# RWKV-7 and chunk-attention block on one core: the solve's transfers on SP's queue, and one gate projection moved ahead

## The chip, the cores and the metric

The kernel runs on one core of a Trainium2 chip. The metric is device time in microseconds (us). The kernel before took 875.37 us (median of 3 runs, 874.01 to 878.43). The profile is one further execution of 873.35 us, of which the trace spans 871.6 us; 1.75 us lie around the span. All times "at 354.65" are us from the start of that span.

Engines: PE is the matrix engine (TensorE), DVE VectorE, ACT ScalarE, POOL GpSimd, SP the engine that does nothing but issue transfers. A transfer is issued by an instruction in the queue of SP or of ACT; an engine works its instructions off in order, so one that waits holds up all behind it.

## The reference

One layer of a residual block for 256 tokens of width 2048. The parts that matter here:

```
h = rms_norm(x)                                   # 256 x 2048
p_r, p_k, p_v, z_r, q, k, v, z_a, m_r, m_a = split(h @ w_in)
# branch 1, RWKV-7, 16 heads of 64: per token and head
sa    = state @ (-kk)
state = state * w + outer(sa, kk * a) + outer(v, k)
y     = state @ r
y_r   = (group_norm(y) * g + b + bonus) * silu(z_r)
# branch 2: attention in chunks of 64 with a relative bias, 16 heads
y_a   = attention(q, k, v) * silu(z_a)
merged = sigmoid(m_r + b0) * (y_r @ w_branch_rwkv) + sigmoid(m_a + b1) * (y_a @ w_branch_attn)
out    = x + rms_norm(merged @ w_out)
```

## The kernel before, in words

**Products.** Nearly all the work is a list of matrix products (`plan`), each read from HBM in weight chunks of 512 KB. `run_plan` walks the chunks. For each, SP loads `raw_*` (3 buffers), ACT copies it to `wh_*` (its high part, L81), DVE subtracts to get `wl_*` (the low part, L82; 4 buffers each), and PE multiplies both into an accumulator `acc_*` in PSUM. There are two accumulators, so a product can start only when that of the product before the last has been taken out (L383 on ACT, then L384 on DVE).

A product for a pair of 128 columns has four chunks. The names: `k`, `r`, `v` with a number are RWKV's inputs; `zr` its gate; `q`, `ak`, `va` the attention's inputs; `za` its gate. The number (0, 2, 4, 6) is the first 128-column tile j0, so `zr4` belongs to the third pair, and `raw_q23` in the order below is chunk 3 of q2. Then follow four rounds of `mr`, `ma`, `ur`, `ua` (merge gates and branch projections) and `o`. The string `ORDER` lists the products between `v6` and the merge: `z` stands for za, `v` for va, `q` for q and ak together, `r` for zr.

**The recurrence.** The 16 heads are two groups of eight; 256 tokens are four chunks of 64. `duo_front` prepares pairs; `group_back(g)` does the rest of a group:

- the solve: an inverse of (I - A) per head and chunk, first in 16 x 16 blocks. Eight small transfers of 16 KB put the diagonal blocks into `nb` in HBM (L577), one brings them back as `N` with another layout (L579), DVE forms the inverse row by row in `S` (15 steps, L590 and L592), one transfer writes `rb` (L595), and eight write the blocks into `R`, part of the tile `RA` (L599). Then come DVE's transpose `T` (L607) and PE's `z` (L611), DVE's `Z` (L615), PE's `xx` (L619), and a second level of the same (`z2`, `x2`; L628, L637).
- the chain over the four chunks c: on PE `pw` (L658, L662), `pu` (L668), `pg` (L682), `py` (L677, L685); on ACT `W`, `UV` and `Y` (L664, L671, L696); on DVE half of `UV` (L670) and the state `SB` (L693, L695).
- the group norm of `Y`.

The first solve falls at 142 to 199 us of the trace, the second at 317 to 379.

**What waits for what.** The q and ak of the third and fourth pair are taken into the tile `late`, which uses the memory of `A` of group 1; so they cannot be taken before group 1's chain has read `A` for the last time (L685 of the last chunk). The gate zr4 is taken into a tile of its own and has no such condition; it is multiplied with `Y` later (`gate`, L785).

**The order.** The code is written in generators (`side`, `back`) that are stepped after each chunk (`pump`), and then a scheduler that estimates times orders the instructions of every engine anew; what it gave is fixed in the program. What it gave is shown below. The engines run their queues in that order.

Of the kernel before, what the change touches and what calls it, by code (L numbers as in the profile page):

```python
# [32 lines left out]
FIRST = ((0, 2), (2, 2))  # L33


ORDER = "q0 r2 v0 z0 v1 r6 r0 z2 q2 q4 q6 z4 r4 z6"

P = 128
D = 2048
# [22 lines left out]
def kernel(ctx: ExitStack, tc, x, xt, vecs, w_in, wa1, w2, a2, w0, rel, w_br, w_ba, w_out, post_g, bm, out):  # L62
    nc = tc.nc
# [405 lines left out]
    def duo_front(j0):  # L469
# [92 lines left out]
        if q0:  # L562
            back.append(group_back(g))
            if g:
                back.append(start_att())

    def group_back(g):
        d = G[g]
        AB, A, UV = d["AB"], d["A"], d["UV"]
        Au = A.rearrange("p h j c a t -> p h (j c) a t")  # L570

        nb = dr.tile([2, 4, 16, 16, 16], F32, tag="nb", name=f"nb{g}")
        rb = dr.tile([2, 4, 16, 16, 16], F32, tag="rb", name=f"rb{g}")
        for h in range(2):
            for b in range(4):
                p0 = 64 * h + 16 * b
                nc.scalar.dma_start(nb[h, b].rearrange("u i j -> i u j"), Au[p0:p0 + 16, h, :, 0, 16 * b:16 * b + 16])  # L577
        N = tp.tile([P, 16, 16], F32, tag="Z2", name=f"N{g}", bufs=3)
        nc.scalar.dma_start(N.rearrange("p i j -> p (i j)"), nb.rearrange("h b u i j -> (h b u) (i j)"))  # L579
        S = tp.tile([P, 16, 16], F32, tag="Z2", name=f"S{g}", bufs=3)  # L580
        pr = tp.tile([P, 256], F32, tag="kk", name=f"pr{g}")
        POOL.memset(S, 0.0)
# [1 line left out]
        R = RA[0][:, 0:DB].rearrange("p (u t) -> p u t", u=16)  # L584
        POOL.memset(R, 0.0)
        yield
        for i in range(14, -1, -1):
# [4 lines left out]
            DVE.tensor_reduce(S[:, i, i + 1:16], pv, axis=AX.X, op=ALU.add)  # L592
            if i % 5 == 0:
                yield
        nc.scalar.dma_start(rb.rearrange("h b u i j -> (h b u) (i j)"), S.rearrange("p i j -> p (i j)"))  # L595
        for h in range(2):
            for b in range(4):
                p0 = 64 * h + 16 * b
                nc.scalar.dma_start(R[p0:p0 + 16, :, 16 * b:16 * b + 16], rb[h, b].rearrange("u i j -> i u j"))  # L599
        yield  # L600

        Rq = [R[:, q * 8:q * 8 + 8, :] for q in range(2)]
# [107 lines left out]
        for q in range(2):  # L710
            for m in range(2):
                jj = 2 * q + m
                j = 4 * g + jj
# [51 lines left out]
    def project_rkv(j0):  # L765
        def fresh():
            if j0 == 4:
                G[1] = group_new(1)
                side.append(group_decay(1))
        project(f"k{j0}", O_K + j0 * P, lambda acc: rkv(j0, 1)(acc), quota=QF, before=fresh, act=h_raw if j0 == 2 else h_norm)  # L770
        project(f"r{j0}", O_R + j0 * P, lambda acc: rkv(j0, 0)(acc), quota=QF)
        project(f"v{j0}", O_V + j0 * P, lambda acc: rkv(j0, 2)(acc), quota=QF)
# [150 lines left out]
    project_rkv(6)  # L923
    for what in ORDER.split():
        {"z": project_za, "v": project_va, "q": project_qk, "r": project_zr}[what[0]](int(what[1]))
# [152 lines left out]
```

## Time and profile before

| | us |
|---|---|
| median of 3 runs | 875.37 |
| profiled execution, whole | 873.35 |
| its span | 871.6 |
| PE busy | 846.0 (97% of the span) |
| DVE busy | 572.0 (66%) |
| ACT busy | 424.5 (49%) |
| POOL busy | 17.3 (2%) |

How to read it: PE is busy for all but about 25 us of the span. The busy time is a sum over stages; what a change to the order can move are the gaps in PE's row, and the stretches in which PE runs on a lower clock. Rows of the timeline give start, duration, engine, line and operation, and in brackets the idle time before and what ended it. A row with the engine `ACTq` or `SPq` is an instruction that issues a transfer.

### The profile page before, as it was taken

The page shows a single profiled execution, that of the slowest core. Times are in us where ns is not written, and L with a number is a line of the kernel's source. Part 1 is how long each engine was busy: PE and PEld are TensorE (multiplying, and loading weights), DVE is VectorE, ACT ScalarE, POOL GpSimd, SP SyncE. Part 2 cuts the span into 40 slices and gives each one's busy share as a digit, 9 for nine tenths or more (in the row PEclk, how much of TensorE's full clock was granted, in tenths as well). Part 3 has the DMA queues.
Part 4 walks back from the last instruction along what each step waited for, and adds up shares of the span by engine and source line. Part 5 has one row for each costly group of instructions (what it writes and reads, how often), then busy time and mean ns, then how long its engine had stood idle before and what let it go on. Part 6 is the DMA issues. An engine that isn't in the chain of part 4 may idle for free.

```text
span 871.6 us, 13996 instructions
## 1 busy us (share of the span) xinstructions
PE 846.0 (97%) x5624; PEld 716.5 (82%) x5624; DVE 572.0 (66%) x801; ACT 424.5 (49%) x600; POOL 17.3 (2%) x68
## 2 busy tenths in 40 slices
PE   8999999999999999899899999999999999999996
PEld 8998888888878888778687777888888888888896
DVE  7897995966548968544597774555564565555554
ACT  7557565446335545243456664444444444434442
POOL 2010000000010000000000000000000000000000
PEclk9999999999899999999999999999999999999999
DMA  9916644654243546534265445666666667675552
GB/s 294 252 53 181 191 138 142 193 159 124 76 141 98 186 145 212 180 101 133 86 188 164 132 129 176 209 195 198 205 193 200 208 194 230 209 260 198 194 192 97
DMA packets 119395, 149.35 MB, mean 171 GB/s; under 512 B 13601, under 2 KB 82209, under 8 KB 118946
## 3 DMA queue, kind: packets, MB, share of 16 engines
q1 hardware_dynamic: 105090, 138.43, 50.2%
q10 hardware_dynamic: 14240, 10.03, 4.0%
q8 instruction: 44, 0.72, 0.3%
q14 instruction: 21, 0.17, 0.1%
HBM read 145.82 MB, written 2.62 MB: 170 GB/s over the span
## 4 chain that ended last, share of the span: by engine, by line
PE 54%; DVE 1%; ACT 0%; DVEq 0%; issue 0%
PE acc_mr L275 10%; PE acc_ma L275 10%; PE acc_o L275 9%; PE acc_ua L275 5%; PE acc_ur L275 5%; PE acc_q L339 2%; PE acc_za L339 2%; PE acc_ak L339 2%; PE acc_q L337 1%; PE acc_za L337 1%; PE acc_ak L337 1%; PE acc_zr L339 1%; PE po L862 1%; PE acc_last L275 1%; PE pT L854 1%; PE pS L829 1%
## 5 line engine op out<-in xcount | busy, mean ns | idle before, releaser
L275 PE MATMUL acc_mr<-wh_mr,hn 128*128 128x512 f32 x256 | 82.0, 394 | 0.0
L275 PE MATMUL acc_ma<-wh_ma,hn 128*128 128x512 f32 x256 | 79.5, 389 | 0.0
L82 DVE TENSOR_TENSOR wl_ma<-raw_ma,wh_ma 128x1024 fp32r<-128x1024 f32 x32 | 39.2, 1224 | 42.3 <-ACT wh_ma L81 42.3
L82 DVE TENSOR_TENSOR wl_o<-raw_o,wh_o 128x1024 fp32r<-128x1024 f32 x31 | 37.9, 1225 | 32.9 <-ACT wh_o L81 32.9
L82 DVE TENSOR_TENSOR wl_mr<-raw_mr,wh_mr 128x1024 fp32r<-128x1024 f32 x32 | 39.1, 1223 | 28.8 <-ACT wh_mr L81 28.8
L275 PEld LDWEIGHTS acc_mr<-wh_mr,hn 128*128 128x128 f32 x256 | 47.8, 188 | 10.7 <-issue 1.2
L81 ACT ACTIVATE wh_ma<-raw_ma 128x1024 fp32r<-128x1024 f32 x32 | 34.0, 1061 | 46.3 <-PE acc_mr L275 20.9
L275 PEld LDWEIGHTS acc_ma<-wh_ma,hn 128*128 128x128 f32 x256 | 48.0, 188 | 10.0
L81 ACT ACTIVATE wh_mr<-raw_mr 128x1024 fp32r<-128x1024 f32 x32 | 33.9, 1060 | 43.3 <-PE acc_ua L275 19.9
L81 ACT ACTIVATE wh_o<-raw_o 128x1024 fp32r<-128x1024 f32 x31 | 32.9, 1060 | 39.0 <-PE acc_o L275 28.0
L275 PE MATMUL acc_mr<-wl_mr,hn 128*128 128x512 f32 x128 | 50.1, 392 | 0.0
L275 PE MATMUL acc_o<-wh_o,mgh 128*128 128x512 f32 (+1 forms) x140 | 49.9, 356 | 0.0
L275 PE MATMUL acc_o<-wl_o,mgh 128*128 128x512 f32 (+1 forms) x140 | 49.8, 356 | 0.0
L275 PE MATMUL acc_ma<-wl_ma,hn 128*128 128x512 f32 x128 | 49.8, 389 | 0.0
L275 PE MATMUL acc_va<-wh_va,hn 128*128 128x512 f32 x128 | 41.0, 398 | 0.0
L339 PE MATMUL acc_q<-hn,wh_q 128*128 128x512 f32 x128 | 33.8, 399 | 3.2 <-DVE late L384 1.7
L339 PE MATMUL acc_ak<-hn,wh_ak 128*128 128x512 f32 x128 | 33.9, 401 | 1.5 <-DVE aq L384 1.5
L339 PE MATMUL acc_za<-hn,wh_za 128*128 128x512 f32 x128 | 33.9, 398 | 0.0
L339 PE MATMUL acc_zr<-hn,wh_zr 128*128 128x512 f32 x128 | 33.3, 397 | 0.0
L82 DVE TENSOR_TENSOR wl_ua<-raw_ua,wh_ua 128x1024 fp32r<-128x1024 f32 x16 | 19.6, 1223 | 20.5 <-ACT wh_ua L81 20.5
L81 ACT ACTIVATE wh_ak<-raw_ak 128x1024 fp32r<-128x1024 f32 x16 | 16.7, 1056 | 31.5 <-PE acc_q L339 13.9
L82 DVE TENSOR_TENSOR wl_ur<-raw_ur,wh_ur 128x1024 fp32r<-128x1024 f32 x16 | 19.6, 1223 | 17.9 <-ACT wh_ur L81 17.9
(481 smaller groups left out, 2101.9 us busy)
## 6 DMA issues: line engine op xcount, KB each, us to landing
raw_mr<-w_in_d SPq DMA_DIRECT2D x32, 512.0 KB, 4.4
raw_ma<-w_in_d SPq DMA_DIRECT2D x32, 512.0 KB, 4.5
raw_o<-w_out_d SPq DMA_DIRECT2D x32, 512.0 KB, 3.7
raw_v<-w_in_d SPq DMA_DIRECT2D x16, 512.0 KB, 3.7
raw_q<-w_in_d SPq DMA_DIRECT2D x16, 512.0 KB, 4.6
raw_ak<-w_in_d SPq DMA_DIRECT2D x16, 512.0 KB, 3.7
raw_zr<-w_in_d SPq DMA_DIRECT2D x16, 512.0 KB, 3.7
raw_va<-w_in_d SPq DMA_DIRECT2D x16, 512.0 KB, 3.6
```

Source lines behind the costliest of these rows:

```text
L81: ACT.activation(h, src, AF.Copy)
L82: DVE.tensor_tensor(l, src, h.bitcast(F32), op=ALU.subtract)
L275: PE.matmul(d, u, v, start=first and n == 0, stop=last and n == len(ops) - 1)
L337: PE.matmul(acc[:, m, 0:256], wl[:, k, ms], a[:, 0, :], start=False, stop=g == ng - 1 and k == 3)
L339: PE.matmul(acc[:, m, :], wh[:, k, ms], a.rearrange("p n t -> p (n t)"), start=g == 0 and k == 0, stop=False)
L829: PE.matmul(pS[h][:, 128:384], q[HS[h], m, 128:256], k[HS[h], m, :], start=True, stop=True)
L854: PE.transpose(pT[:, b * P:(b + 1) * P], S[:, h, b * P:(b + 1) * P], ident)
L862: PE.matmul(po[m][HS[h], 128 * n:256], va[n][:, vc], att[1][:, 2 * m + h, c0:c1], start=not n, stop=bool(n))
```

## The change

It consists of two edits. The 18 transfers of each solve (`nb` x8, `N`, `rb`, `RA` x8) are issued by SP and no longer by ACT. And in `ORDER` the gate `r4` (product zr4, four chunks) stands ahead of q4 and ak4, where it stood between za4 and za6.

```
-ORDER = "q0 r2 v0 z0 v1 r6 r0 z2 q2 q4 q6 z4 r4 z6"
+ORDER = "q0 r2 v0 z0 v1 r6 r0 z2 q2 r4 q4 q6 z4 z6"
...
-                nc.scalar.dma_start(nb[h, b].rearrange("u i j -> i u j"), Au[p0:p0 + 16, h, :, 0, 16 * b:16 * b + 16])
+                nc.sync.dma_start(nb[h, b].rearrange("u i j -> i u j"), Au[p0:p0 + 16, h, :, 0, 16 * b:16 * b + 16])
...
-        nc.scalar.dma_start(N.rearrange("p i j -> p (i j)"), nb.rearrange("h b u i j -> (h b u) (i j)"))
+        nc.sync.dma_start(N.rearrange("p i j -> p (i j)"), nb.rearrange("h b u i j -> (h b u) (i j)"))
...
-        nc.scalar.dma_start(rb.rearrange("h b u i j -> (h b u) (i j)"), S.rearrange("p i j -> p (i j)"))
+        nc.sync.dma_start(rb.rearrange("h b u i j -> (h b u) (i j)"), S.rearrange("p i j -> p (i j)"))
...
-                nc.scalar.dma_start(R[p0:p0 + 16, :, 16 * b:16 * b + 16], rb[h, b].rearrange("u i j -> i u j"))
+                nc.sync.dma_start(R[p0:p0 + 16, :, 16 * b:16 * b + 16], rb[h, b].rearrange("u i j -> i u j"))
```

The scheduler gives a new order on all engines from the first solve on. Up to the first solve, and between the end of the first chain and the second solve, the order of PE is the one of before.

SP's queue at the second solve (`raw_q2x` and `raw_ak2x` are weight chunks of the products q2 and ak2):

```order
 L90 DMA raw_q22_4162<-w_in_d 128x4x256
 L90 DMA raw_q23_4185<-w_in_d 128x4x256
+L595 DMA rb1_2809<-S1_2820 128x256
+L599 DMA RA_848<-rb1_2809 16x16x16 x8
 L90 DMA raw_ak20_4207<-w_in_d 128x4x256
 L90 DMA raw_ak21_4229<-w_in_d 128x4x256
 L90 DMA raw_ak22_4254<-w_in_d 128x4x256
```

All four loads of ak2 now stand behind the nine transfers of the solve. At the first solve the pattern is nearly the same: rb, then raw_q02, then the eight RA, then raw_q03; and `nb` stands ahead of raw_r61, `N` behind it. On ACT these 36 rows are gone.

PE at the same place, the product q2 (chunks q20 to q23) with the solve's z and xx in between:

```order
 L339 MATMUL acc_q2_4166<-hn_656,wh_q21_4132 128x512 x8
 L337 MATMUL acc_q2_4166<-hn_656,wl_q21_4133 128x256 x8
+L611 MATMUL z10_2914<-T10_2912,A1_1878 64x64 x16
+L611 MATMUL z11_2933<-T11_2931,A1_1878 64x64 x16
 L339 MATMUL acc_q2_4166<-hn_656,wh_q22_4160 128x512 x8
 L337 MATMUL acc_q2_4166<-hn_656,wl_q22_4161 128x256 x8
-L339 MATMUL acc_q2_4166<-hn_656,wh_q23_4183 128x512 x8
-L611 MATMUL z10_2914<-T10_2912,A1_1878 64x64 x16
-L611 MATMUL z11_2933<-T11_2931,A1_1878 64x64 x16
-L337 MATMUL acc_q2_4166<-hn_656,wl_q23_4184 128x256 x8
+L339 MATMUL acc_q2_4166<-hn_656,wh_q23_4183 128x512 x2
 L619 MATMUL xx10_2974<-RA_848,Z10_2972 64x64 x16
```

The z of the second solve now stands after the second chunk of q2, where it stood in the fourth; xx comes after two matmuls of the fourth chunk, and z2 and the first of x2 move from within ak2 to ahead of it. At the first solve z moves ahead of the first chunk of q0, where it stood after five of its matmuls. On DVE, the last of the solve's 15 steps (`S`, L592) now stands ahead of the gate zr0 (L785) and of wl_q21; two chunks of wl_ak2 stand between `T` and `Z`, where three did.

PE at the end of group 1's chain, before (the last chunk of ak4 is just over):

```order
L658 MATMUL pw13_3389<-UV1_1879,A1_1878 64x64 x5
L662 MATMUL pw13_3389<-SB_162,AB10_1231 64x64 x4
L662 MATMUL pw13_3389<-SB_162,AB11_1232 64x64 x4
L668 MATMUL pu13_3408<-W13_3406,RA_848 64x64 x8
L677 MATMUL py13_3437<-AB10_1231,SB_162 64x64 x4
L677 MATMUL py13_3437<-AB11_1232,SB_162 64x64 x4
L685 MATMUL py13_3437<-A1_1878,UV1_1879 64x64 x8
L339 MATMUL acc_q6_4617<-hn_656,wh_q60_4565 128x512 x8
```

The same place in the changed kernel:

```order
L339 MATMUL acc_ak4_4624<-hn_656,wh_ak42_4618 128x512 x2
L668 MATMUL pu13_3408<-W13_3406,RA_848 64x64 x8
L677 MATMUL py13_3437<-AB10_1231,SB_162 64x64 x4
L677 MATMUL py13_3437<-AB11_1232,SB_162 64x64 x4
L339 MATMUL acc_ak4_4624<-hn_656,wh_ak42_4618 128x512 x6
L337 MATMUL acc_ak4_4624<-hn_656,wl_ak42_4619 128x256 x8
L339 MATMUL acc_ak4_4624<-hn_656,wh_ak43_4641 128x512 x6
L685 MATMUL py13_3437<-A1_1878,UV1_1879 64x64 x8
L339 MATMUL acc_ak4_4624<-hn_656,wh_ak43_4641 128x512 x2
L337 MATMUL acc_ak4_4624<-hn_656,wl_ak43_4642 128x256 x8
L705 MATMUL pvr10_3457<-ysq10_3455,onesb_108 128x256 x2
L339 MATMUL acc_q6_4715<-hn_656,wh_q60_4663 128x512 x8
```

Before, the chain's last chunk (names that end in 13) runs with no matmuls of a product in between; now its pieces stand between those of ak4. What follows is the same work with one product less: the attention of the third and fourth pair moves over into mr0 and ma0 by about the length of a product, and the last `po` (L862) from the end of mr0 into the first half of ma0.

## The prediction

> **What bounds the kernel now.** I read the page's busy times first, then the waits of PE, then the timeline of PE where it waits, then ACT, DVE and the transfers at those places.
>
> ```profile
> PE 846.0 (97%) x5624; PEld 716.5 (82%) x5624; DVE 572.0 (66%) x801; ACT 424.5 (49%) x600; POOL 17.3 (2%) x68
> ```
>
> ```profile
> PE pw L662 <- DVE SB L695: 3.2, 2, 2.2
> ```
>
> PE is idle for 25 us of 871.6, and the change neither adds nor removes a matmul. So the time moves only with PE's gaps behind the first solve, and with its clock. The head, up to 140 us, is untouched. The timeline of PE shows the gaps:
>
> ```profile
> 354.65 2.00 PE L339 MATMUL acc_q<-hn,wh_q 128*128 128x512 f32 x8
> ...
> 357.44 2.00 PE L339 MATMUL acc_q<-hn,wh_q 128*128 128x512 f32 x8
> 359.93 2.08 PE L611 MATMUL z<-T,A 64*64 64x64 f32 x64 [0.49 <-DVE T L607]
> ...
> 364.55 2.28 PE L619 MATMUL xx<-RA,Z 64*64 64x64 f32 x64 [1.39 <-issue]
> 368.35 2.14 PE L339 MATMUL acc_ak<-hn,wh_ak 128*128 128x512 f32 x8 [1.52 <-DVE aq L384]
> ...
> 386.62 2.12 PE L339 MATMUL acc_q<-hn,wh_q 128*128 128x512 f32 x8 [1.49 <-DVE ak L384]
> ...
> 408.83 0.69 PE L662 MATMUL pw<-SB,AB 128*64 128x64 f32 x16
> ...
> 420.45 1.13 PE L662 MATMUL pw<-SB,AB 128*64 128x64 f32 x16 [1.02 <-DVE SB L695]
> 422.05 0.68 PE L668 MATMUL pu<-W,RA 64*64 64x64 f32 x16 [0.47 <-ACT W L664]
> ...
> 426.03 2.11 PE L339 MATMUL acc_q<-hn,wh_q 128*128 128x512 f32 x8 [1.69 <-DVE late L384]
> ```
>
> Three groups: the second solve loses 0.49 + 1.39 + 1.52 = 3.40 us. The start of q4 loses 1.49. The end of the chain loses 1.02 + 0.47 + 1.69 = 3.18, and 0.44 more, as the pw of the last chunk takes 1.13 where it takes 0.69 between matmuls of a product. Why the second solve is late stands in the rows of ACT and DVE:
>
> ```profile
> 344.81 0.40 ACTq L818 DMA_DIRECT2D E<-rel_d  x1
> ...
> 346.30 0.33 ACTq L595 DMA_DIRECT2D rb<-S  x1
> ...
> 352.31 5.01 ACTq L599 DMA_DIRECT2D RA<-rb  x8
> 357.42 2.95 ACT L81 ACTIVATE wh_ak<-raw_ak 128x1024 fp32r<-128x1024 f32 x3 [8.00 <-DMA RA<-rb]
> ...
> 424.66 0.59 ACT L383 ACTIVATE late<-acc_q 128x512 f32<-128x512 f32 x1
> ...
> 425.62 1.16 ACT L702 ACTIVATE ysq<-Y 128x512 f32<-128x512 f32 x2
> ```
>
> ```profile
> 344.10 0.68 DVE L785 SCALAR_TENSOR_TENSOR zr<-Y,zr 128x512 f32<-128x512 f32 x1
> 344.70 1.22 DVE L82 TENSOR_TENSOR wl_q<-raw_q,wh_q 128x1024 fp32r<-128x1024 f32 x1
> 345.83 0.38 DVE L592 TENSOR_REDUCE S<-pr 128x15 f32<-128x225 f32 x1
> ...
> 359.17 1.30 DVE L607 STREAM_TRANSPOSE T<-RA 128x512 f32<-128x512 f32 x2 [8.49 <-DMA RA<-rb]
> 360.40 3.45 DVE L82 TENSOR_TENSOR wl_ak<-raw_ak,wh_ak 128x1024 fp32r<-128x1024 f32 x3
> ```
>
> The solve's inverse is done at 346.2, rb is issued at once, and RA waits 6 us for it to land, right behind the 512 KB of E on the same queue. ACT stands for 8.00 us with three copies wh_ak behind it. DVE stands for 8.49 us, then works off three wl_ak ahead of Z, for which xx waits. The transfers at both solves, the first from the window 165 to 182 us, the second from 344 to 360:
>
> ```profile
> raw_q<-w_in_d SPq DMA_DIRECT2D x4, 512.0 KB, 4.8
> rb<-S ACTq DMA_DIRECT2D x1, 128.0 KB, 3.2
> ```
>
> ```profile
> raw_ak<-w_in_d SPq DMA_DIRECT2D x3, 512.0 KB, 5.6
> E<-rel_d ACTq DMA_DIRECT2D x1, 512.0 KB, 5.7
> rb<-S ACTq DMA_DIRECT2D x1, 128.0 KB, 6.0
> ```
>
> **The change part by part. Second solve.** In the new order the last step of S stands ahead of the gate (0.68) and wl_q (1.22), so S ends at about 344.3. The nb are issued at the same time as before (they wait for A, not for a queue), so I leave the rest of the chain up to S alone. On SP, rb has raw_q23 ahead of it and E is on the other queue. How long rb takes there no row shows; I take the first solve's 3.2, where rb also had a raw_q in flight; the ends are 3.2 and 6.0. RA can then be issued at 347.5; eight take 5.0 us (352.31 row) and end at 352.5; T came 1.85 us after the last issue (359.17 - 357.32), so now at about 354.6, with the spread of my sum about 355. Half of T (0.65) is enough for the first z.
>
> PE reaches z earlier, since z now stands after the second chunk: at 354.65. It waits till 355.7, 1.0 us. Then z (2.08), chunk three (2.8, from 354.65 to 357.44) and two matmuls of the fourth (0.5): xx at 361.0.
>
> The price of the move is on SP: all behind RA waits. The loads of ak2 go out at 352.5 and no longer at 346 to 351. The first lands after about 4 us, the three within 5.6, so at 356.5 to 358.5; two copies of 1.06 and two wl of 1.23 later Z starts at about 360.3 and has its first half at 361.0. That is just in time: I put 0.5 us of waiting there. The take of aq still stands behind the fourth copy wh_ak on ACT, whose load needs the buffer of the first; so ak2 still waits, I say 1.0 us of the 1.52. Together 2.5 against 3.40: **0.9 us gained**. Ends: all gaps gone, 3.4 gained; or rb takes its 6.0 and T stays at 359.17: then z waits 5.2, and 2.8 us are lost.
>
> **Start of zr4 (before: of q4).** It needs the accumulator of ak2. In the old order nothing stood between, and PE waited 1.49. Now pg, py and the first pw of chunk 1 stand between, three times 16 small matmuls, 1.8 us at the 0.6 to 0.7 us that 16 take (408.83 row). ACT and DVE take ak2 in that time, after wl_zr43 (1.23) and with 0.69: 1.9 us. What is left is 0.2 to 0.3: **1.2 us gained**; ends 0 and 1.49.
>
> **End of the chain.** zr4 puts 11.2 us of matmuls (four chunks of 2.8) in front of q4, and its accumulator empties without waiting for `late`. So the last chunk of the chain runs between matmuls of ak4, and SB, W and UV have 2 us and more each. After the last py ten matmuls of ak4 are left (1.4 us); in that time ACT does Y, then late (0.59) and the first ysq (half of 1.16), and DVE its half of late (as long as the 0.68 of another 512-wide operation); pvr then covers the rest. I leave 0.3 us of waiting: 3.18 + 0.44 - 0.3 = **3.3 us gained**. Ends: 1.5, if late and ysq come in turn (1.69 stays), and 3.6.
>
> **First solve.**
>
> ```profile
> 151.78 0.16 DVE L590 TENSOR_TENSOR pr<-S,N 128x1 f32<-128x1 f32 x1 [1.68 <-DMA N<-nb]
> ...
> 180.44 1.30 DVE L607 STREAM_TRANSPOSE T<-RA 128x512 f32<-128x512 f32 x2 [1.22 <-DMA RA<-rb]
> ```
>
> ```profile
> 180.03 1.33 PE L339 MATMUL acc_q<-hn,wh_q 128*128 128x512 f32 x5
> 181.28 2.08 PE L611 MATMUL z<-T,A 64*64 64x64 f32 x64
> ```
>
> PE now reaches z at 180.03, 1.25 us earlier, and T was there at 181.1 (its first half). ACT no longer holds copies and takes behind nb, so S starts up to 1.7 us earlier and T comes at about 179.0 to 179.4: no wait. I take 0; if N and RA lose what they gain behind raw_r61 and raw_q02, z waits 1.1; if besides rb takes 6.0 instead of 3.2, 3.9. After this solve comes the longest gap, and the clock with it:
>
> ```profile
> 218.80 1.57 PE L662 MATMUL pw<-SB,AB 128*64 128x64 f32 x16 [2.16 <-DVE SB L695]
> ```
>
> ```profile
> 218.00:220.00 2.00, 1.14 (x15) 0.73 0.65 231
> 220.00:222.00 2.00, 1.53 (x24) 0.50 0.00 0
> 222.00:224.00 2.00, 2.00 (x37) 0.50 0.04 8
> 224.00:226.00 2.00, 2.00 (x34) 0.56 0.00 0
> ```
>
> Columns: length, PE busy (instructions), granted clock, transfers. 2 x (0.27 + 0.50 + 0.50 + 0.44) = 3.4 us are lost to the clock. DVE's work ahead of that SB (duo_front of the third pair) is the same in sum and merely swapped with wl_zr23, so gap and clock stay: 0, with 3.4 gained if the gap falls just short.
>
> **Cover.** All else that moves to SP costs nothing: 36 issues of 0.3 to 0.6 us while SP waits for buffers anyway; what hides it are three raw and four wh buffers, some 2.8 us each. The later attention is hidden as long as the last po and the gate of mr0 come before ur0.
>
> ```profile
> 528.38 0.87 PE L862 MATMUL po<-att_yrh,va 128*64 128x256 f32 x8
> ...
> 554.02 0.39 PE L275 MATMUL acc_ur<-wh_ur,yr_AB 128*128 128x512 f32 x1
> ```
>
> They are 25 us apart; the move takes some 11 to 14 of them.
>
> **Sum.** 0.9 + 1.2 + 3.3 = 5.4 us: the profiled execution's 873.35 would become 868.0, and the median of 875.37, which lies 2.0 above it, 870.0. About 0.5% (4.4 us) is what a measurement of this kernel can tell from no change.
>
> **A page's rule against the change.** That rb took 6.0 us behind E's 512 KB and 3.2 without is a row of this trace. The Trainium skill ("DMA: Bandwidth & Descriptors", Queues, rings and completion order) states that SP and ACT each own a row of rings on the same 16 engines, that a ring is worked in order and the engines take turns between rows. By that the solve's transfers lose their turns against the weight loads once they share SP's row, and it agrees with the 6.0 us. By it rb and RA would wait for the raw_q ahead of them, up to 4.8 us at each solve, and the sum would turn into the rival that follows.
>
> **The rivals.** *Solve stuck in SP's queue (slower).* Place: rb and RA of both solves behind raw_q23, raw_q01 and raw_q02. Price: with 6.0 for rb at both, 2.8 lost at the second and 3.9 at the first, and a z wait of 5.2 is longer than the 2.16 that brought the clock down, 3.4 more: 10.1 against the 4.5 of the other two terms, 5.6 slower, 881. It decides from T coming some 2.5 us later than I say at both solves. For it: the 6.0. Against: rb at the first solve had loads in flight and took 3.2, and at the second SP's queue holds one load, where ACT's held E. Its weaker form, only the second solve, costs 2.8, leaves 4.5 - 2.8 = 1.7 gained: 873.7, no change.
>
> *The clock keeps up at 219.* The gap is shorter by a few tenths and the drop does not come: 3.4 more, 866.6. For it: the gap is short. Against: nothing on DVE's path there gets less. The Trainium skill ("TensorE: Matmul & The Clock Gate", The HAM clock gate) puts the drop at one idle window of about 3.4 us; here 2.16 us of idling with another 0.47 behind it did it, so here the clock falls sooner than by the page, and I go by the trace.
>
> *zr4 does not help.* The chain's end stays bare, as DVE or ACT is late with SB or UV for another reason; then 3.3 becomes 0 to 1: 872.5. Against: the old gaps are there only where no product stands between.
>
> **How the numbers follow.** Forecast (4.4 to 8 gained) 0.50; clock kept too 0.09; one of the weaker cases (second solve gives back its part, or the chain's end half as good) 0.31; solve stuck at both 0.10. That gives faster 0.59, same 0.32, slower 0.09. Predicted 870.0; the likeliest case alone 867.5 to 871. The range 865.5 to 876 takes in the kept clock below and the weaker cases above, with the spread of the three runs.
>
> **What would show it.** Right: in the changed profile PE's wait at acc_q for late is below 0.5, no pw of the last chunk waits for SB, acc_zr starts with under 0.5, T of the second solve comes 3 to 5 us earlier and the wait of ACT for RA is gone. Wrong: z waits for T by more than 2 us, raw_ak or raw_q03 shows up as a releaser of PE, or a second stretch of half clock stands near 356.

## The result, and the profile after

The changed kernel took 863.21 us (median of 4 runs, 862.21 to 864.87), the kernel before 874.69 beside it (4 runs, 873.36 to 878.43): a ratio of 0.987, with a 95% interval of 0.985 to 0.989, so 1.3% or 11.5 us faster. The profiled executions differ by 9.83 us (873.35 and 863.52); the reading below accounts for those. I had forecast a gain of 5.4.

The page's line of busy times, then PE's waits behind the first solve:

```profile
PE 842.4 (98%) x5624; PEld 714.7 (83%) x5624; DVE 572.6 (66%) x801; ACT 425.4 (49%) x600; POOL 17.2 (2%) x68
```

```profile
PE pw L662 <- DVE SB L695: 1.8, 1, 1.8
...
PE pu L668 <- ACT W L664: 0.5, 1, 0.5
...
PE acc_ak L339 <- DVE aq L384: 0.3, 1, 0.3
PE acc_zr L339 <- DVE ak L384: 0.3, 1, 0.3
```

Two things are to be seen. The waits around the second solve and at the end of the second chain are gone but for 0.2 or 0.3 here and there; pw and pu are the gap behind the first solve, at 216.7, which stayed. And PE's busy time fell by 3.6 us with the same 5624 matmuls. My prediction allowed only for the 0.44 of one pw. Of the 3.6, 1.0 lies ahead of q2, where PE waits 1.3 us longer in this trace and nothing is gained; 2.8 lie between the starts of q6 and ur0, and these are gain; from q2 to q6 it rose by 0.2.

PE at the places of the prediction:

```profile
349.38 2.00 PE L339 MATMUL acc_q<-hn,wh_q 128*128 128x512 f32 x8
...
355.06 2.08 PE L611 MATMUL z<-T,A 64*64 64x64 f32 x64
...
360.53 2.19 PE L619 MATMUL xx<-RA,Z 64*64 64x64 f32 x64
...
367.40 2.08 PE L339 MATMUL acc_ak<-hn,wh_ak 128*128 128x512 f32 x8 [0.30 <-DVE aq L384]
...
385.02 2.14 PE L339 MATMUL acc_zr<-hn,wh_zr 128*128 128x512 f32 x8 [0.26 <-DVE ak L384]
...
428.06 0.69 PE L685 MATMUL py<-A,UV 128*64 128x64 f32 x16
...
431.01 2.21 PE L339 MATMUL acc_q<-hn,wh_q 128*128 128x512 f32 x8
...
445.96 2.00 PE L339 MATMUL acc_ak<-hn,wh_ak 128*128 128x512 f32 x8
...
544.26 0.39 PE L275 MATMUL acc_ur<-wh_ur,yr_AB 128*128 128x512 f32 x1
```

They are the starts of q2, z, xx, ak2, zr4, the last py, q6, ak6 and ur0. The starts of q2 and ak6 before, which are not shown yet:

```profile
349.06 2.00 PE L339 MATMUL acc_q<-hn,wh_q 128*128 128x512 f32 x8
...
442.19 2.00 PE L339 MATMUL acc_ak<-hn,wh_ak 128*128 128x512 f32 x8
```

Aligned at equal work (what PE has done more or less by then is added; zr4 is 11.17 us), the gain builds up as follows:

| from, to | gained, us | forecast |
|---|---|---|
| up to the start of q2 (the head differs from run to run) | -0.3 | 0 |
| q2 to the start of zr4: 386.62 against 385.02 (1.6), plus pg, py and pw, done by then (1.8), plus the 0.3 of the row above | 3.7 | 0.9 + 1.2 |
| to the start of q6: 426.03 against 431.01, zr4 and four pvr (0.8) done | 3.6 | 3.3 |
| to the start of ak6: 442.19 + 11.17 against 445.96 | 0.4 | 0 |
| to the start of ur0: 111.83 - 11.17 = 100.66 us before, 98.30 after | 2.4 | 0 |
| to the end | 0.0 | 0 |

The second solve on the transfers' side (DVE, SP, ACT; the numbers at the end of the last two rows are KB of one transfer and us from issue to landing):

```profile
343.82 0.38 DVE L592 TENSOR_REDUCE S<-pr 128x15 f32<-128x225 f32 x1
...
344.28 0.34 SPq L595 DMA_DIRECT2D rb<-S  x1
...
344.83 0.39 ACTq L818 DMA_DIRECT2D E<-rel_d  x1
...
347.87 3.77 SPq L599 DMA_DIRECT2D RA<-rb  x8
...
351.74 6.89 SPq L90 DMA_DIRECT2D raw_ak<-w_in_d  x4
...
353.60 1.30 DVE L607 STREAM_TRANSPOSE T<-RA 128x512 f32<-128x512 f32 x2 [2.60 <-DMA RA<-rb]
...
355.92 1.06 ACT L81 ACTIVATE wh_ak<-raw_ak 128x1024 fp32r<-128x1024 f32 x1 [6.18 <-DMA raw_ak<-w_in_d]
...
359.65 1.28 DVE L615 TENSOR_TENSOR Z<-z,m 128x512 f32<-128x512 f32 x2
```

```profile
rb<-S SPq DMA_DIRECT2D x1, 128.0 KB, 3.5
...
RA<-rb SPq DMA_DIRECT2D x8, 16.0 KB, 2.1
```

S ends at 344.20 and T starts at 353.60: 9.4 us, where it was 13.0 before (346.21 to 359.17). The raw_ak now go out behind RA; ACT waits 6.18 us for the first and DVE 2.11 for ACT's copy of it, but PE waits for neither.

### The profile page after: what moved, and what is told of

It reads as the page before. It is cut to its first block, busy times and chain, and to the rows that moved or that the text cites. A ratio compares the mean times of both kernels' runs of the same rounds, so it can differ in the third digit from the quotient of the medians.

```text
span 861.8 us, 14000 instructions
## 1 busy us (share of the span) xinstructions
PE 842.4 (98%) x5624; PEld 714.7 (83%) x5624; DVE 572.6 (66%) x801; ACT 425.4 (49%) x600; POOL 17.2 (2%) x68
## 4 chain that ended last, share of the span: by engine, by line
PE 93%; DVE 2%; DMA 2%; SPq 1%; issue 0%; ACT 0%; DVEq 0%
PE acc_mr L275 10%; PE acc_ma L275 10%; PE acc_o L275 10%; PE acc_va L275 5%; PE acc_ua L275 5%; PE acc_ur L275 5%; PE acc_zr L339 4%; PE acc_q L339 4%; PE acc_za L339 3%; PE acc_ak L339 3%; PE acc_v L339 3%; PE acc_r L339 3%; PE acc_za L337 2%; PE acc_zr L337 2%; PE acc_q L337 2%; PE acc_k L339 2%
## 5 line engine op out<-in xcount | busy, mean ns | idle before, releaser
L275 PEld LDWEIGHTS acc_ma<-wh_ma,hn 128*128 128x128 f32 x256 | 47.8, 188 | 10.1 <-issue 0.3
L82 DVE TENSOR_TENSOR wl_va<-raw_va,wh_va 128x1024 fp32r<-128x1024 f32 x16 | 19.5, 1222 | 17.2 <-ACT wh_va L81 15.8
```

The source lines that it names most:

```text
L82: DVE.tensor_tensor(l, src, h.bitcast(F32), op=ALU.subtract)
L275: PE.matmul(d, u, v, start=first and n == 0, stop=last and n == len(ops) - 1)
```

## The experiments

Times are medians beside the kernel before on the same chip; ratios are to it, with their 95% intervals. Times of stretches are of one profiled execution each. "Stretch" is the start of ak6 to the start of ur0, without zr4 where it lies in it.

**1. The two edits one at a time.** First the order alone:

```
-ORDER = "q0 r2 v0 z0 v1 r6 r0 z2 q2 q4 q6 z4 r4 z6"
+ORDER = "q0 r2 v0 z0 v1 r6 r0 z2 q2 r4 q4 q6 z4 z6"
```

> Only the order of the products is changed (zr4 ahead of q4); the solve's transfers stay on ACT. From the two traces the 9.8 us between them split into 2.7 at the second solve, 1.0 at the start of zr4, 3.6 at the end of the chain and 2.4 between the first ak6 and the first ur0, less 0.3 lost in the head. Theory one (order and queue add up, and the 2.4 belong to the order, as no pair of po stands split by a product any more): gains 1.0 + 3.6 + 2.4 = 7.0, so about 867.5 if the kernel before takes 874.5; ak6 to ur0 takes about 98.5 to 99.5 us without zr4's 11.2; E still stands ahead of rb on ACT and T of the second solve waits for RA. Rival (the 2.4 and part of the cover come from the transfers leaving ACT): gains 4.5 at most, 870, and ak6 to ur0 takes 100.7 without zr4. Rival two (the earlier zr4 is worth nothing while the solve stays on ACT): 873 to 875.

Measured 871.14 against 874.13, 0.9948 (0.9924 to 0.9972). PE's waits:

```profile
PE acc_q L339 <- DVE late L384: 1.7, 1, 1.7
PE acc_ak L339 <- DVE aq L384: 1.7, 1, 1.7
PE acc_zr L339 <- DVE ak L384: 1.5, 1, 1.5
```

Then the queue alone (the four lines `nc.scalar` to `nc.sync` of the change, with the old `ORDER`):

> Only the queue of the solve's transfers is changed to SP; the old order of products stays. Theory one: gains the second solve's 2.7 and nothing else, so about 871.8 against 874.5; rb of the second solve lands in 3.2 to 3.6 us in place of 6.0; the po pairs stay split and ak6 to ur0 keeps its 111.8 us. Rival (the transfers lose their turns behind the weight loads on SP): rb takes 5 us or more and the time is 874.5 or above. Rival two (the interleaving at the end comes from SP): 869.5 and ak6 to ur0 takes 109.5.

Measured 869.68 against 874.13, 0.9956 (0.9934 to 0.9978). PE's waits and the transfer:

```profile
PE acc_q L339 <- DVE late L384: 1.7, 1, 1.7
PE acc_ak L339 <- DVE aq L384: 0.3, 1, 0.3
PE acc_q L339 <- DVE ak L384: 0.3, 1, 0.3
```

```profile
rb<-S SPq DMA_DIRECT2D x1, 128.0 KB, 3.3
```

Neither theory fits whole. From the start of q2 to that of ur0 the order alone gains 3.7 us, the queue alone 5.3, both 10.1. The wait of 1.5 for ak2's take, which I had given to the order, goes with the queue: as the solve ends earlier, pg, py and pw of the chain stand ahead of the next product, whichever it is. The wait of 1.0 for SB at the chain's end goes with either edit, the wait for `late` only with both. With the order alone the last py stands behind all of ak4, which is over at 432.30, and ends at 432.92; with the queue alone no product is left either. Only an earlier chain and one product more give the ten matmuls of ak4 behind the last py; this I read from the orders, no run tries it by itself. The stretch takes 98.78 us with the order alone and 100.66 with the queue alone: that gain is the order's, as I had said.

**2. Why rb took 6.0 us.** My guess was E's 512 KB ahead of it on the same queue. So E goes to the other queue, in the kernel before:

```
-        nc.scalar.dma_start(E, bass.AP(rel.tensor, 2 * j0 * 513 + 129, [[1, P], [513, 4], [1, T]]))
+        nc.sync.dma_start(E, bass.AP(rel.tensor, 2 * j0 * 513 + 129, [[1, P], [513, 4], [1, T]]))
```

> The kernel before with one edit: the four loads E of the attention's bias (512 KB each) are issued by SP; the solve stays on ACT in the old order. Theory one (rb took 6.0 us because E stood ahead of it on the same queue): rb of the second solve lands in 3.2 to 3.8 us, T comes 2.2 to 2.8 us earlier (about 356.7), the waits of 0.49, 1.39 and 1.52 shrink by 2 us or more: 872 to 872.8 against 874.5. Rival (the 16 DMA engines were busy, whichever queue): rb stays at 5 to 6 us and the time at 874.5. Rival two (what costs is that ACT stands behind RA, not rb's landing): rb is faster but the gain is under 0.7.

Measured 873.59 against 874.13, 0.9995 (0.9978 to 1.0012), and:

```profile
rb<-S ACTq DMA_DIRECT2D x1, 128.0 KB, 5.9
```

The guess was wrong. Next, less traffic, again in the kernel before:

```
-        nc.scalar.dma_start(E, bass.AP(rel.tensor, 2 * j0 * 513 + 129, [[1, P], [513, 4], [1, T]]))
+        nc.scalar.dma_start(E[:, 0:4 if j0 else 1, :], bass.AP(rel.tensor, 2 * j0 * 513 + 129, [[1, P], [513, 4 if j0 else 1], [1, T]]))
```

> The kernel before, with the first E load cut from 512 to 128 KB: the first attention's four heads all take the bias of the first of them; nothing else is left out. With E on SP rb still took 5.9 us, so the queue ahead of rb is not its cause. Theory one (the traffic of two 512 KB loads in flight, E and the first raw_ak, slows rb whatever the queue): with one of them cut rb of the second solve lands in 3.5 to 4.5 us, T comes 1.5 to 2.5 us earlier, and 1 to 2 us are gained: 872 to 873 against 874. Rival (raw_ak alone is enough to slow rb, or ACT's queue is slow by itself): rb stays at 5.5 us or more, no gain.

Measured 873.77 against 874.56, 0.999 (0.9965 to 1.0015): rb became shorter as the first theory has it, but T came only 0.9 us sooner after the end of S, and no gain can be told. And the changed kernel, with RA alone back on ACT:

```
-                nc.sync.dma_start(R[p0:p0 + 16, :, 16 * b:16 * b + 16], rb[h, b].rearrange("u i j -> i u j"))
+                nc.scalar.dma_start(R[p0:p0 + 16, :, 16 * b:16 * b + 16], rb[h, b].rearrange("u i j -> i u j"))
```

> The changed kernel, with the eight RA loads of both solves issued by ACT again; nb, N and rb stay on SP. SP then no longer waits for rb and sends the four raw_ak right behind it. Theory one (what helps is that SP, in order, holds the raw_ak back until RA is out, so that rb and RA have the DMA engines nearly to themselves): rb takes 4.5 us or more at the second solve, RA is issued later than 348.5 less the shift of the head, eight issues take 5.0 instead of 3.8 us, and T comes 1.5 to 4 us later than in the changed kernel; 1 to 4 us of the gain are lost, 864.5 to 867. Rival (a small transfer is fast on SP, whatever runs beside it): rb 3.5, T within 1.3 us of the changed kernel's, and as wh_ak then no longer waits for its loads the time is 862.5 to 863.5.

Measured 866.38 against 874.56, 0.992 (0.9897 to 0.9943): some 2 to 3 us lost, as the first theory has it, but with an rb of 3.3 and not of 4.5 or more. The transfers of the second solve, first with a quarter of E, then with RA on ACT:

```profile
rb<-S ACTq DMA_DIRECT2D x1, 128.0 KB, 4.2
```

```profile
rb<-S SPq DMA_DIRECT2D x1, 128.0 KB, 3.3
RA<-rb ACTq DMA_DIRECT2D x4, 16.0 KB, 5.0
```

| kernel | in flight as rb is issued (us since their issue) | rb, us | last RA issue to T | end of S to T |
|---|---|---|---|---|
| before (rb on ACT) | E (1.5) on ACT, raw_ak (0.4) on SP | 6.0 | 1.9 | 13.0 |
| E on SP (rb on ACT) | E (1.5) and raw_ak (0.4) on SP | 5.9 | 1.7 | 12.8 |
| a quarter of E (rb on ACT) | 128 KB (1.5) on ACT, raw_ak (0.4) on SP | 4.2 | 3.3 | 12.1 |
| RA on ACT (rb on SP) | raw_q (1.4) on SP | 3.3 | 3.3 | 12.3 |
| queue alone | raw_q (1.4) on SP | 3.3 | 2.0 | 9.2 |
| changed | raw_q (1.4) on SP | 3.5 | 2.0 | 9.4 |

For rb, what decides is what was issued just ahead of it, and not on which queue: 6.0 and 5.9 with E on either, and 3.5 on SP right behind a load on SP. A load that follows rb counts less: in the three rows with rb on SP, E goes out on ACT 0.55 us behind rb, and rb still lands in 3.3 to 3.5. The traffic is paid for at rb or at RA: with a quarter of E, or with RA on ACT, the raw_ak that are then in flight go with a later landing of RA (3.3). It is paid least where SP, which works in order, stands at rb and RA and so holds the raw_ak back. RA on ACT releases them, and T comes 2.9 us later than in the changed kernel: 1.3 of that is the landing, and 1.9 that the eight issues take 5.66 us on ACT where they took 3.77 on SP. Whether ACT or the traffic makes the issues longer, no run separates. Of the gain, 1.7 us are lost between q2 and ur0 (1.0 against the second trace of the changed kernel, below). At the first solve and chain nothing is lost: from the start of v6 to that of va0 PE takes 72.53 us, and 72.65 in the changed kernel. The rest of the difference between the two medians I can't place.

**3. Where the busy time went.** In the old order PE's block of `po` was cut between its two heads at two places; in the new one it isn't. Before, at one of them:

```profile
486.34 0.65 PE L862 MATMUL po<-att_yrh,va 128*64 128x256 f32 x2
486.91 0.48 PE L827 MATMUL pS<-late 64*128 64x128 f32 x2
487.33 0.86 PE L862 MATMUL po<-att_yrh,va 128*64 128x256 f32 x6
```

The same block in the changed kernel:

```profile
484.88 0.87 PE L862 MATMUL po<-att_yrh,va 128*64 128x256 f32 x8
```

First try: the same eight matmuls, one head written behind the other.

```
-            for n, c0, c1 in ((0, 0, 256), (1, 256, 384)):
-                for h in range(2):
+            for h in range(2):
+                for n, c0, c1 in ((0, 0, 256), (1, 256, 384)):
```

> The changed kernel, with the two heads' po matmuls of a block written one head after the other, so that their two 64-row halves no longer follow each other directly. In the trace of before two of the eight blocks were cut between the halves by another matmul, and took 0.57 and 0.79 us, 1.36 together, where the uncut ones take 0.80. Theory one (two halves that follow each other directly run side by side, and each cut costs its 0.5 to 0.6 us on PE, which shows as busy time and not as a wait): eight blocks cost 0.5 to 0.6 more each, 4 to 5 in all: 867 to 868 against the changed kernel's 863.2; mr0 to ur0 gets longer and PE's busy time rises by as much. Rival (the lengths of such records are a matter of how ends are drawn, or the lost time is taken back in waits): within 1 us of 863.2.

Measured 864.94, 0.9897 (0.9875 to 0.9919), stretch 98.36: no difference from the changed kernel that can be told.

```profile
463.18 0.88 PE L862 MATMUL po<-att_yrh,va 128*64 128x256 f32 x8
```

The order of the heads is not what costs, as long as nothing comes in between. So the next kernel makes something come in between. The changed kernel stands beside it once more:

> The changed kernel itself, run beside the next two so that they can be compared with it on one chip: 863.2 against 874.5 for the kernel before, a ratio of 0.985 to 0.989; ak6 to ur0 98.3 us, T of the second solve 9.4 us after the end of S, as in its first trace.

Measured 864.12 against 874.75, 0.9878 (0.9855 to 0.9901); stretch 98.30. In this second trace z and xx of the second solve wait 0.3 and 0.5, where they waited for nothing in the first. The cut kernel (`turn_half` holds the transposes and the copy of one head; its definition, and the first head's call at the old place of the transposes, are left out here):

```
-            for n, c0, c1 in ((0, 0, 256), (1, 256, 384)):
-                for h in range(2):
+            for h in range(2):
+                if h:
+                    turn_half(m, 1)
+                for n, c0, c1 in ((0, 0, 256), (1, 256, 384)):
```

> The changed kernel, with each attention step's second head transposed (pT) only behind the first head's po matmuls, so that every po block falls in two pieces with product matmuls between, and pS and pT in smaller pieces too: 89 places where PE goes from one kind of matmul to another between the first ak6 and the first ur0, where the changed kernel has 47 and the old order 52. The matmuls themselves are the same. Before, the same stretch took 100.66 us with the old order (zr4's 11.17 taken off), 98.30 in the changed kernel, 98.78 with the order alone; writing the heads one behind the other without a cut cost nothing (98.36). Theory one (each cut costs PE some 0.2 us for a pS block and 0.5 to 0.6 for a po block, and stands as busy time, not as a wait): the stretch takes 103 to 108 us, and the kernel 867 to 873 against 863.2. Rival (the 2.4 us were two places where PE waited for something that the records do not show): 98 to 100 us, the kernel within 1.5 us of the changed one.

Measured 876.3, 1.0019 (1.0006 to 1.0031): 12 us slower than the changed kernel. Everything up to ak6 is at the same place (445.63); the stretch takes 111.23, of which 1.31 is a wait of ur0 for the attention. PE's rows of po and pS:

```profile
464.56 0.86 PE L865 MATMUL po<-att_yrh,va 128*64 128x256 f32 x4
...
470.71 0.48 PE L832 MATMUL pS<-ak,aq 64*128 64x128 f32 x2
471.04 0.59 PE L834 MATMUL pS<-ak,aq 64*128 64x256 f32 x2
```

And pS in the changed kernel:

```profile
488.44 0.49 PE L827 MATMUL pS<-late 64*128 64x128 f32 x4
488.76 0.60 PE L829 MATMUL pS<-late 64*128 64x256 f32 x4
```

Four matmuls of one head take 0.86 us, eight of both heads 0.87; two of pS 0.48, four 0.49. The heads lie in different halves of the array and run side by side when they follow each other, and a head that stands alone costs as much as both. If each matmul's time is taken from its start to the start of the next, less waits, po goes from 6.4 to 12.8 us and pS from 7.1 to 10.2; of the 11.6 in all, 2.7 more lie in the products in between, and pT, the transposes, takes 0.6 less. The Trainium skill ("TensorEngine Tiling (Array Packing)", Tiling Modes) states that tiles of the array run independently, and that a change of the tiling mode drains it. The rows agree with the first. For the second I made a test that counts changes: blocks as long as they can be.

```
-        for m in range(2):
+        for m in (1, 0):
             S = att[0][:, 2 * m:2 * m + 2, :]
-            for h in range(2):
+            for h in (1, 0):
                 pT = small(f"pT{j0 + m}{h}")
```

> The changed kernel, with the transposes pT of an attention step written with the half that is ready last first, so that the others follow it at once and the po of all four halves after them: between the first ak6 and the first ur0 PE goes 30 times from one kind of matmul to another, where the changed kernel does so 47 times and the kernel with every po cut 89 times; pS falls into three pieces in place of two. The matmuls are the same. Theory one (each change of kind costs PE time: 42 more of them cost 12.9 us, 0.31 each): the stretch takes 93 to 97.5 us in place of 98.30 (5.3 less if all 17 are worth 0.31, under 1 less if only the po blocks' ends count), and the kernel 859 to 863 against the changed kernel's 864. Rival (what cost 12.9 us in that kernel were only the two halves of po apart from each other, and blocks of whole halves gain nothing): 98 to 98.8, no difference from the changed kernel.

Measured 866.51 against 874.61, 0.9905 (0.9879 to 0.9931); the stretch takes 100.25, of which 2.14 is a wait for the last gate: 98.1 without it, as in the changed kernel. (The profiled execution is the longest of the six, 873.65; in the stretch its clock is full.)

```profile
476.61 1.52 PE L862 MATMUL po<-att_yrh,va 128*64 128x256 f32 x16
...
552.62 0.50 PE L275 MATMUL acc_ur<-wh_ur,yr_AB 128*128 128x512 f32 x1 [2.14 <-DVE g L967]
```

The rival is right for the time: with 17 changes of kind less, po took 0.5 us less and the products 0.8 less, and pS, in three pieces, and pT took 0.6 more each. What costs is the head alone and hardly the change: by an estimate from the products' matmuls of these two runs (0.8 for 17, 2.7 for 42) a change is worth 0.05 to 0.07 us. Of the 2.4 us between the old order and the new, two cut po are 1.1 and pS in three pieces in place of two 0.6, together 1.7; 0.25 lies in pT and 0.2 in zr4's own matmuls, which took 11.39 in that stretch and not 11.17. Why pT differs stays open.

**4. The gap that stayed.** At 216.7 PE waits for SB, and then its clock is halved for 6.8 us. How long it is halved is not fixed by the gap. The same 12 us, in the trace of the changed kernel and in that of the kernel with one head's po written behind the other's, which differs only behind that place (length; busy time of PE, PEld, DVE, ACT, POOL; granted clock; DMA share; GB/s):

```profile
217.00:229.00 12.00, 9.65 (x113) 8.49 (x114) 8.88 (x17) 3.63 (x7) 0.00 (x0) 0.72 0.15 45
```

```profile
217.00:229.00 12.00, 8.34 (x126) 6.81 (x125) 9.92 (x19) 3.94 (x8) 0.00 (x0) 1.00 0.15 45
```

Both wait 1.82 us for SB and 0.47 for W. The first then loses 0.28 of 12 us, 3.4 us; the second loses nothing. The second trace of the changed kernel has 0.72 there again; the queue alone and the cut po, with the same two waits, have 0.86. So one trace alone can't tell what an edit does to this clock.

Here zr2 goes ahead of q0, as zr4 went ahead of q4:

```
-ORDER = "q0 r2 v0 z0 v1 r6 r0 z2 q2 r4 q4 q6 z4 z6"
+ORDER = "r2 q0 v0 z0 v1 r6 r0 z2 q2 r4 q4 q6 z4 z6"
```

> The changed kernel with zr2 moved ahead of q0 as well, as zr4 was moved ahead of q4. In the changed kernel the first group's chain ends bare of products: waits of 1.8, 0.5 and 0.2, and then 6.8 us at about half the clock, 3.4 lost. Theory one (a product whose accumulator empties without waiting covers the chain's end there too): all of it goes, 5.9 us, 857.3 against 863.2; the granted clock between 215 and 230 is 1.0. Rival (the products are only moved, and the gap comes back at another place of the first chain, or at ak0, whose destination is held till the third pair's front is done): 0 to 2 gained, 861 to 863, with a wait of acc_ak or pw over 1 us between 205 and 235.

Measured 866.97 against 874.13, 0.9919 (0.9896 to 0.9942): no gain on the changed kernel, and by the medians some 3 us slower. The start of q2, and PE's waits behind it:

```profile
343.45 2.00 PE L339 MATMUL acc_q<-hn,wh_q 128*128 128x512 f32 x8
```

```profile
PE acc_ak L339 <- DVE aq L384: 2.4, 1, 2.4
PE acc_q L339 <- DVE late L384: 1.7, 1, 1.7
```

The first half came as expected: no gap, full clock, q2 5.9 us earlier (3.4 of them the clock's). But each step of a chain that runs between product matmuls comes behind them: the last pu of the first chain starts at 260.62 and not at 250.76. The nb of the second solve go out at 329.84 and not at 317.75, T comes at 366.37 and not at 353.60, and 7.9 us are lost from q2 to ur0, 1.7 of them to a clock that is halved behind the wait of 2.4. A second order, with r4 ahead of q2 (`"r2 q0 v0 z0 v1 r6 r0 z2 r4 q2 q4 q6 z4 z6"`):

> As the kernel with zr2 ahead of q0, and zr4 ahead of q2 in place of q4. With zr2 ahead of q0 the first chain's end was covered (q2 began 5.9 us earlier), but each of its steps then waited behind product matmuls, the second solve came 12.8 us later, and 7.9 us were lost from q2 on. Theory one (a covered chain ends later, and the products behind it wait for what it holds): the wait of 2.4 for aq goes, as one product more stands ahead of q2, the wait for late (1.7) and pu (0.5) stays: 863.5 to 865 against 867.0, about level with the changed kernel's 863.2. Rival (the second chain, too, gets covered and the whole 5.9 stays): 858 to 860. Rival two (the accumulators block elsewhere): 867 or above.

Measured 867.15, 0.9927 (0.991 to 0.9945): no better, rival two; the waits are 2.4 and 1.7 again, the first now for zr.

Last, the gap itself. DVE's front of the third pair stands ahead of SB; two of its operations go to POOL (the lines that take the factor 0.5 into account ahead of it are left out here):

```
-            DVE.scalar_tensor_tensor(ab(2 + h, HS[h]), ch(kk, HS[h]), 0.5, iv[HS[h]], op0=ALU.mult, op1=ALU.mult)
+            (POOL.tensor_tensor(ab(2 + h, HS[h]), ch(kk, HS[h]), iv[HS[h]], op=ALU.mult) if j0 == 4 else DVE.scalar_tensor_tensor(ab(2 + h, HS[h]), ch(kk, HS[h]), 0.5, iv[HS[h]], op0=ALU.mult, op1=ALU.mult))
```

> The changed kernel, with one pair of operations of the third pair's front (AB<-kk,iv, 1.39 us on DVE at 215.0) moved to POOL; its factor of a half is folded into the root ahead of it. The order on all other engines stays. In the changed kernel DVE reaches SB 1.8 us after PE has gone idle at 216.7, and PE then runs at about half its clock for 6.8 us. Theory one (DVE's front stands ahead of SB, and the drop of the clock follows from that idle time): SB starts 1.4 us earlier, the wait of pw falls to about 0.4, and as the idle time is then 0.9 in place of 2.3 the clock does not drop: 1.4 + 3.4 = 4.8 gained, 858.4 against 863.2. Rival (the clock drops for the little work in that stretch, not for the one wait): 1.4 gained, 861.8, still 6.8 us at half clock. Rival two (POOL takes DVE's time at the port they share, or is so slow that the later front waits): 0 or a loss.

Measured 865.49, 0.99 (0.9882 to 0.9919): no gain. DVE in the changed kernel, then DVE, POOL and PE with the edit:

```profile
215.04 1.39 DVE L530 SCALAR_TENSOR_TENSOR AB<-kk,iv 64x512 f32<-64x512 f32 x2
216.44 0.61 DVE L533 TENSOR_SCALAR ta<-ta,hv 128x256 f32<-128x256 f32 x2
```

```profile
216.50 1.64 DVE L533 TENSOR_SCALAR ta<-ta,hv 128x256 f32<-128x256 f32 x2
...
216.62 3.79 POOL L530 TENSOR_TENSOR AB<-kk,iv 64x512 f32<-64x512 f32 x2 [50.41 <-PE acc_ak L337]
...
219.66 1.14 PE L662 MATMUL pw<-SB,AB 128*64 128x64 f32 x16 [1.45 <-DVE SB L695]
```

DVE gives away 1.39 and pays 1.03 of it back: L533 takes 1.64 where it took 0.61 while POOL works beside it. The gap shrinks by 0.4, and the clock falls all the same, for 6.8 us. As it also falls for different lengths behind an unchanged gap, this trace does not decide what makes it fall; it does show that moving the two operations shortens the gap by 0.4 and not by 1.4. No version tried beats the changed kernel.

## Why the prediction was wrong in size, point by point

The direction was right; 863.2 lies below the range, which ended at 865.5. I forecast 5.4 us; between the two traces the gain is 9.8, and between the medians 11.5, as the profiled execution before lay below its median. Of the 4.4 that are missing between the traces, 2.8 are busy time, 1.6 the second solve with the start of zr4, and 0.3 the chain's end, less 0.3 in the head.

- **"The time moves only with PE's gaps behind the first solve, and with its clock."** This is the step that failed outright. Between q6 and ur0 PE gains 2.8 us without a wait or a change of clock, as its busy time there falls: 1.9 of it is po and pS, matmuls of one head that now run beside those of the other; the other 0.9 lies in pT, in pvr and in the products' matmuls, and its cause is not shown. It was to be read before: two pS rows of one head and four of both had the same duration. I had read the attention's move as "hidden", and put its term at nothing.
- **Second solve, 0.9.** Mis-sized: the waits of 0.49, 1.39 and 1.52 became 0, 0 and 0.3, with 0.2 at an x, so 2.9 gained (2.1 in the second trace). T came at 353.60, where I had put 355, as the eight RA took 3.77 us to issue and not 5.0; PE came to z at 355.06, so nothing waited. The price on SP that I had put at 1.5 us came to 0.5: raw_ak came in time for Z. The reason I gave for the 6.0 of rb, E's place on ACT's queue, was wrong. It was E and raw_ak issued in the last 1.5 us ahead of it, on whichever queue, and SP's order is what keeps raw_ak out.
- **Start of zr4, 1.2.** The size is right (1.49 became 0.26), the cause is not: this came with the queue and not with the order.
- **End of the chain, 3.3.** Right, 3.6, but I had it from the order alone, which leaves the 1.7 for `late`, my lower end.
- **First solve, 0.** Right: T at 179.34, no wait at z, and gap and half clock at 216.7 as before. "The clock keeps up" did not come about in this trace, nor did "zr4 does not help". For the clock that is partly luck: I had it follow from the gap, and the trace with a clock of 1.00 behind the same two waits shows that it need not.
- **Solve stuck in SP's queue.** It did not come about. The Trainium skill ("DMA: Bandwidth & Descriptors", Queues, rings and completion order) has a ring worked in order and the engines take turns between the queues. That the traffic counts, with E on either queue, agrees with it, and rb did stand behind a raw_q on SP. Only the price was another: that load had a start of 1.4 us, so rb took 3.5 and not the 6.0 of the rival.

## What to carry to other kernels

Before a transfer that a chain waits for, ask what else is in flight; a queue that works in order can hold large loads back just by standing at the small one, and that can be worth more than their earlier arrival. A reordering also changes which small matmuls stand next to each other: look for blocks whose halves run side by side, and count those that get cut, for their cost is PE busy time and no wait shows it. Two edits around one chain are to be measured one at a time: here each alone left a wait that only both took away, and covering the first chain with a product made the second one late. Where a clock drops behind a gap, look at it in several traces before an edit gets the credit.

## What the runs showed of the hardware

- Two heads' matmuls that use different halves of the array take the time of one: 0.87 us for eight and 0.86 for four (po), 0.49 for four and 0.48 for two (pS).
- A 128 KB transfer (rb) landed in 2.7 to 3.7 us with the last 512 KB load 1.3 to 1.4 us ahead of it on its own queue, in 4.1 and 4.8 with that load 0.5 us ahead (the two kernels with zr2 ahead of q0), and in 5.9 to 6.2 with two such loads in the last 1.5 us, on one queue or on two.
- A pair of DVE operations (L533) of 0.61 us took 1.64 beside a POOL operation. The Trainium skill ("SBUF — State Buffer", SBUF: two separate sides) has the two engines share one pair of ports, which the whole instruction locks; the 1.03 us more agree with that, though no run shows that L533 takes this pair.
- PE's clock after waits of 1.82 and 0.47 us was halved for about 6.8 us in both traces of the changed kernel, for 3.4 with the queue alone and with the cut po, and not at all with one head's po behind the other's; after 1.45 and 0.47, with the edit for POOL, for 6.8. At the end of the second chain, behind waits of 1.02, 0.47 and 1.69, it stayed full in the kernel before and was halved for 3.4 us in the one with a quarter of E.
